# A hybrid decoder step on one core: the first FFN operands on two engines in another order, more products ahead of them, the last output parts in one contraction

## The chip, the core and the metric

One NeuronCore of a Trainium2 chip runs the whole program. The core has four engines that compute, each with its own queue of instructions that it works off in order: TensorE (PE; its weight loads are shown as PEld), VectorE (DVE), ScalarE (ACT) and GpSimd (POOL). SyncE (SP) issues nearly all transfers. Matrix products go into PSUM, eight banks of 512 fp32 columns per partition; everything else lies in SBUF.

The metric is the device time of one execution in microseconds. The profile is of one further execution, whose own time is given beside the median of the others.

## The reference

One layer on 2048 prompt tokens and 8 decode tokens, model width 1024, FFN width 2816:

```python
h = rmsnorm(x, g_mix) * (1.0 + scale_m) + shift_m
proj = h @ w_in                      # q, k, v, g_ret, x_lru, g_lru
...
mix = jnp.concatenate([ret_out, lru_out], axis=-1) @ w_out
x = x + gate_m * mix

h = rmsnorm(x, g_ffn) * (1.0 + scale_f) + shift_f
u = h @ w_up_conv
gv = h @ w_up_gate
uc, s_conv_ffn_new = causal_dwconv(u, s_conv_ffn, conv_ffn_w, conv_ffn_b)
f = (jax.nn.gelu(uc) * gv) @ w_down
x = x + gate_f * f
```

Between `proj` and `mix` stand four retention heads (a chunkwise recurrence, 128 tokens a chunk) and an RG-LRU over 512 channels. `scale`, `shift` and `gate` are `silu(c) @ w_ada + b_ada`. The recurrent states are outputs too, and a last `rmsnorm` follows.

## The kernel before

**Numbers.** Every fp32 factor of the large products is split into a high part (the value rounded to the type `fp32r`, by ACT) and a low part (the rest, a subtraction), and a product is three matmuls: high·high, high·low, low·high. This is `mm3` (lines 346, 347, 348); all three lines appear in the profile for every product. The split weights are made once, in the first token group, by `parts` (ACT line 277, POOL line 278), stored to DRAM and loaded from there by the later groups.

**Groups and blocks.** The tokens are worked in three groups of 688, 680 and 688 columns (the last has the 8 decode tokens), each cut in two blocks of 344 (or 340). Activations lie transposed: channels on partitions, tokens along the free dimension. A group runs: projection (`head(p)`, `lru(t)`), retention (`ret`, in steps between other work), output projection (`out_(p)`), the second norm (`norm2`), FFN up and gate products, down projection (`dn`).

**FFN up and gate by seven products.** For a pair of 128-column output tiles and the two token blocks, the 2×2 block product of weights (A11, A12 | A21, A22) and activations is done by seven block products instead of eight. With b11, b21 the two halves of the channels (k below 4 and above) in block 0, and c12, b22 those of block 1:

- t1 = c12 − b11, t2 = b22 − t1, t3 = t2 − b11, t4 = b21 − t2
- P1 = A11·b11, P2 = A12·b21, P5 = S1·t1, P6 = S2·t2, P7 = S3·t3, P3 = S4·b22, P4 = A22·t4

where S1 to S4 are sums of the A. P1 and P2 need block 0 alone. The others need both blocks. Some products are added up in one PSUM bank (`qx`: P1, P6, P7, P4; `qz`: P5, P3; `qy`: P2), and the sums are taken out by ACT or DVE (`keep` line 971, `up_out` lines 1001 and 1003, `gate_out` line 1038). There are 11 pairs of tiles for `w_up_conv` and 11 for `w_up_gate`. One product is four k-steps of `mm3`, 12 matmuls.

**Where the operands come from.** After the last output part of a block, `square` and `norm2` make the norm factor: squares on ACT (842), their sum on DVE (845), small matmuls (858), DVE (862), POOL (864), DVE (867), and matmuls that spread the factor over partitions (869). Then `operands1` (block 0) and `operands2` (block 1) copy the factor from PSUM (lines 901, 917) and make the operand tiles `op`. `h2` (883 to 890) applies norm, scale and shift: in way "v" DVE multiplies (889) and ACT adds the shift (890), in way "p" POOL multiplies (886) and ACT scales and shifts (887). `hilo` (892 to 894) makes high parts on ACT (893) and low parts on DVE or POOL (894), as its caller says. The differences are DVE's lines 938, 940, 946 and 949. `raw32` holds b11 and b21 in fp32 for them (tile `keep`).

**Order.** `group_items` writes out the order of the work as a list of items (weight keys, rate, function). `fetch` is called for the keys ahead of use, up to a weight of `LOOK` = 4 blocks, into a ring of 8 blocks (`wb`); raw weights go through 7 buffers (`wr`, `ws`). After each item, generators in `soon` and `bg` (norms, retention steps) are advanced by the item's rate. This order gives priorities; the framework then lays out each engine's queue by a simulated schedule, and on the chip each queue runs in that fixed order. Before the change the end of the output projection runs as 12 items of head 2 and LRU tile 2, then a drain of `bg`, then 8 items of head 3, 4 of head 2 and 8 of head 3. Each item (`down_item`) contracts one head and one LRU tile, 6 matmuls, and is added to x by DVE (820). In front of the rest of the FFN stand four products that need block 0 alone: P1 and P2 of pair 0, for up and gate.

**Pools.** `x` has nine large slots (x, hh, hl, rope, heads, operands), `t` ten tiles of one block, `f` twelve split tiles, `pm` three and `pt` five PSUM banks.

Of the kernel before, what the change touches and what calls it, by code (L numbers as in the profile page):

```python
# [16 lines left out]
P = 128  # L17
# [3 lines left out]
NB = 8  # L21
# [7 lines left out]
HOW0, HOW1, HOW2 = "vmvmvmvm", "pmpmpmpm", "vpvpvpvp"  # L29
# [59 lines left out]
def hybrid_step(ctx: ExitStack, tc: tile.TileContext, I, O):  # L89
# [194 lines left out]
    def fetch(key, r_=None, lo_on=G):  # L284
# [15 lines left out]
        elif kind == "w_down":  # L300

            units[key] = parts(key, block(), None if key in split else load_rows_of(kind, a, 512 * key[2]), lo_on)
        elif kind in ("w_in", "w_out"):
            both = []
            for h in range(2):
                r_ = None
                if key + (h,) not in split:
                    r_ = load_rows_of(kind, a, 512 * h) if kind == "w_out" else load_cols_of(kind, a, h)
                both.append(parts(key + (h,), block(), r_, lo_on))
            units[key] = [(both[k // 4][0][:, k % 4, :], both[k // 4][1][:, k % 4, :]) for k in range(KC)]  # L310
        else:
            fetch_operand(key)

    def fetch_operand(key):
# [25 lines left out]
        if i == 0 and nm in ("A11", "A12"):  # L340
# [83 lines left out]
    def fsplit(src, n, name):  # L424
        hi = fp.tile([P, BMAX], F32R, tag="f", name=name + "h")
        lo = fp.tile([P, BMAX], F32R, tag="f", name=name + "l")
# [17 lines left out]
    class Group:  # L444
        def __init__(g, gi):
# [7 lines left out]
            g.xt, g.rope = {}, None  # L453
            g.started, g.sq, g.cv, g.fft, g.up = set(), {}, {}, {}, {}
# [155 lines left out]
        def ret(g, p):  # L610
# [66 lines left out]
            g.mixt[p] = {b: fsplit(SG[:, b[0]:b[1]], b[1] - b[0], "mr") for b in g.blocks}  # L677
# [66 lines left out]


# [14 lines left out]
        def lru_g(g, t, b):  # L760
# [7 lines left out]
            g.mixt.setdefault(4 + t, {})[b] = fsplit(xc, n, "ml")  # L768
# [39 lines left out]
        def down_item(g, keys, parts, jg, b, m):  # L808
# [3 lines left out]
            for i, key in enumerate(keys):  # L812
                if key[0] == "w_down":
                    wh, wl = (v[:, m % 4, :] for v in units[key])
                else:
                    wh, wl = units[key][m]
# [21 lines left out]
        def square(g, b, k):  # L838
# [4 lines left out]
            if 0 < k < KC - 1:  # L843
                acc = g.sq[b][0]
                V.tensor_tensor(out=acc, in0=acc, in1=t0, op=ALU.add)
            else:
                g.sq.setdefault(b, []).append(t0)
# [33 lines left out]
        def h2(g, k, c, n, bc, out, how):  # L881

            A, B = modv[:, 4, k, 0:1], modv[:, 3, k, 0:1]
            xs, t0 = g.xk(k)[:, c:c + n], out[:, 0:n]
            if how == "p":
                G.tensor_tensor(out=t0, in0=xs, in1=bc[:, 0:n], op=ALU.mult)
                S.activation(out=t0, in_=t0, func=AF.Identity, scale=A, bias=B)
            else:
                V.scalar_tensor_tensor(out=t0, in0=xs, scalar=A, in1=bc[:, 0:n], op0=ALU.mult, op1=ALU.mult)
                S.activation(out=t0, in_=t0, func=AF.Identity, bias=B)  # L890

        def hilo(g, nm, k, src, eng):
            S.activation(out=g.hi(nm, k), in_=src, func=AF.Copy)  # L893
            eng.tensor_tensor(out=g.lo(nm, k), in0=src, in1=g.hi(nm, k).bitcast(F32), op=ALU.subtract)  # L894

        def operands1(g, b, ps):
# [3 lines left out]
            bc = ttile("bc")  # L900
            S.activation(out=bc[:, 0:n], in_=ps[:, 0:n], func=AF.Copy)
# [10 lines left out]
        def operands2(g, b, ps):  # L912
            n, np_ = g.n, g.npr(b)
            for v in ("t1", "b22", "t2", "t4"):
                g.op[v] = slot("op", F32R)
            bc = ttile("bc")
            S.activation(out=bc[:, 0:n], in_=ps[:, 0:n], func=AF.Copy)
            tails, t3s = [], []
            if np_ < n:
                for u in range(2):  # L920
# [403 lines left out]
```

## Time and profile before

| | |
|---|---|
| median of 3 runs | 2508.69 us (2506.72 to 2509.22) |
| the profiled execution, its own time | 2514.42 us |
| span of its instructions | 2512.3 us |
| mean granted clock of TensorE | 0.971 |
| instructions | 40048 |
| busy: PE, DVE, ACT, POOL | 2395.7, 1465.1, 877.4, 840.6 us |
| bytes moved | 523.96 MB, mean 209 GB/s |

The groups' entries into the FFN lie at about 380, 1195 and 2000 us after the span's start. A timeline row has start, duration, engine, line, operation, output<-input, shapes and count; in brackets stands how long the engine was idle before and what ended the idle time. A row of waits has the waiting engine, its tile and line, what it waited for, then the sum, the count and the longest. A row of one line's durations has minimum, median and maximum in ns.

### The profile page before, as it was taken

The numbers are of one execution on the slowest core, as the hardware profiler recorded it, in microseconds if no ns is written. First come the engines' busy times: TensorE is split into PE (matmuls) and PEld (weight loads), VectorE is DVE, ScalarE is ACT, GpSimd is POOL, SyncE is SP. The second block draws the span as 40 slices with busy tenths as digits, with TensorE's granted clock in tenths as the row PEclk, the third lists the DMA queues.
The fourth block names the chain that finished last, engine by engine and source line by source line (L and its number), as shares of the span: only waits on it lengthen the run. The fifth ranks groups of instructions, "written<-read, shape, count | busy, mean of one in ns | idle before, by whom it ended". The sixth has DMA issues, their size and how long they took to land. (4 is left out here: it accounts for less than half of the span.)

```text
span 2512.3 us, 40048 instructions
## 1 busy us (share of the span) xinstructions
PE 2395.7 (95%) x15145; PEld 2293.4 (91%) x15145; DVE 1465.1 (58%) x3121; ACT 877.4 (35%) x1944; POOL 840.6 (33%) x849
## 2 busy tenths in 40 slices
PE   5999996999999999999799999999999979999997
PEld 4988885999999999999699999989999879999997
DVE  3745577676667766567644434376565855454545
ACT  3423446544444443223422222243123442222222
POOL 2544547767666643222311010132222330101011
PEclk8999997999999999999799999999999989999999
DMA  9575654888878854332466666746433245666673
GB/s 342 170 267 192 202 194 165 310 292 291 301 281 302 322 196 140 130 117 95 138 233 233 223 241 218 247 170 196 135 124 129 90 157 211 242 218 236 217 245 129
DMA packets 227777, 523.96 MB, mean 209 GB/s; under 512 B 18493, under 2 KB 100553, under 8 KB 227577
## 3 DMA queue, kind: packets, MB, share of 16 engines
q1 hardware_dynamic: 226483, 520.65, 59.8%
q8 instruction: 119, 1.95, 0.3%
q10 hardware_dynamic: 974, 0.50, 0.1%
q14 instruction: 73, 0.60, 0.1%
q0 software_dynamic: 128, 0.26, 0.0%
HBM read 373.04 MB, written 148.42 MB: 208 GB/s over the span
## 5 line engine op out<-in xcount | busy, mean ns | idle before, releaser
L820 DVE SCALAR_TENSOR_TENSOR x<-down,mod,x 128x344 f32<-128x344 f32 (+2 forms) x720 | 401.0, 569 | 329.9 <-PE down L348 324.7
L428 POOL TENSOR_TENSOR ffl<-cv,ffh 128x344 fp32r<-128x344 f32 (+1 forms) x132 | 132.3, 1009 | 763.9 <-ACT ffh L427 707.9
L346 PE MATMUL proj<-hh,wb 128*128 128x344 f32 (+1 forms) x1152 | 377.5, 328 | 10.1 <-ACT bc L546 7.2
L348 PE MATMUL proj<-hh,wb 128*128 128x344 f32 (+1 forms) x1152 | 371.4, 322 | 0.0
L347 PE MATMUL proj<-hl,wb 128*128 128x344 f32 (+1 forms) x1152 | 370.9, 322 | 0.2 <-DVE hl L559 0.2
L346 PE MATMUL down<-ffh,wb 128*128 128x344 f32 (+1 forms) x1056 | 339.9, 328 | 13.9 <-DVE x L820 13.1
L347 PE MATMUL qx<-op,wb 128*128 128x344 f32 (+1 forms) x1056 | 343.3, 325 | 9.7 <-DVE op L894 6.6
L346 PE MATMUL qx<-op,wb 128*128 128x344 f32 (+1 forms) x1056 | 341.3, 325 | 10.3 <-ACT op L893 6.2
L348 PE MATMUL qx<-op,wb 128*128 128x344 f32 (+1 forms) x1056 | 340.4, 323 | 0.0
L347 PE MATMUL down<-ffl,wb 128*128 128x344 f32 (+1 forms) x1056 | 338.3, 321 | 0.0
L348 PE MATMUL down<-ffh,wb 128*128 128x344 f32 (+1 forms) x1056 | 337.9, 321 | 0.0
L278 POOL TENSOR_TENSOR wb<-wr,wb 128x512 fp32r<-128x512 f32 x170 | 231.8, 1374 | 159.1 <-ACT wb L277 145.0
L346 PEld LDWEIGHTS proj<-hh,wb 128*128 128x128 f32 x1152 | 217.5, 189 | 19.9 <-ACT bc L546 7.3
L347 PEld LDWEIGHTS proj<-hl,wb 128*128 128x128 f32 x1152 | 218.0, 189 | 2.6 <-DVE hl L559 0.7
L346 PEld LDWEIGHTS down<-ffh,wb 128*128 128x128 f32 x1056 | 198.6, 189 | 23.6 <-DVE x L820 22.4
L348 PEld LDWEIGHTS proj<-hh,wb 128*128 128x128 f32 x1152 | 217.6, 189 | 1.7 <-issue 0.9
L347 PEld LDWEIGHTS qx<-op,wb 128*128 128x128 f32 x1056 | 202.7, 192 | 13.8 <-DVE op L894 9.9
L346 PEld LDWEIGHTS qx<-op,wb 128*128 128x128 f32 x1056 | 202.4, 192 | 12.3 <-ACT op L893 6.8
L1023 DVE SCALAR_TENSOR_TENSOR cv<-u,vec,cv 128x344 f32<-128x344 f32 (+2 forms) x264 | 178.4, 696 | 56.9 <-ACT cv L1004 54.3
L348 PEld LDWEIGHTS qx<-op,wb 128*128 128x128 f32 x1056 | 202.5, 192 | 0.1
L347 PEld LDWEIGHTS down<-ffl,wb 128*128 128x128 f32 x1056 | 200.2, 190 | 0.0
L348 PEld LDWEIGHTS down<-ffh,wb 128*128 128x128 f32 x1056 | 200.1, 190 | 0.0
(281 smaller groups left out, 4827.0 us busy)
## 6 DMA issues: line engine op xcount, KB each, us to landing
wb<-w_in SPq DMA_DIRECT2D x96, 512.0 KB
wb<-w_up_conv_S SPq DMA_DIRECT2D x88, 512.0 KB
wb<-w_up_gate_S SPq DMA_DIRECT2D x88, 512.0 KB
wb<-w_down SPq DMA_DIRECT2D x88, 512.0 KB
wb<-w_up_conv_A SPq DMA_DIRECT2D x66, 512.0 KB
wb<-w_up_gate_A SPq DMA_DIRECT2D x66, 512.0 KB
w_in<-wb SPq DMA_DIRECT2D x48, 512.0 KB
w_up_conv_S<-wb SPq DMA_DIRECT2D x44, 512.0 KB
```

The lines of the kernel that those rows point to most:

```text
L278: lo_on.tensor_tensor(out=w[:, 512:1024], in0=src, in1=w[:, 0:512].bitcast(F32), op=ALU.subtract)
L346: T.matmul(out, wh, xh, start=first, stop=False, skip_group_check=more)
L347: T.matmul(out, wh, xl, start=False, stop=False, skip_group_check=more)
L348: T.matmul(out, wl, xh, start=False, stop=last, skip_group_check=more)
L428: G.tensor_tensor(out=lo[:, 0:n], in0=src, in1=hi[:, 0:n].bitcast(F32), op=ALU.subtract)
L820: V.scalar_tensor_tensor(out=xs, in0=q[:, 0:np_], scalar=modv[:, jg, m, 0:1], in1=xs, op0=ALU.mult, op1=ALU.add)
L1023: V.scalar_tensor_tensor(out=cv[:, 0:np_], in0=u[:, j:j + np_], scalar=cfw[:, j, ft:ft + 1], in1=cv[:, 0:np_], op0=ALU.mult, op1=ALU.add)
```

## The change

`operands1` and `operands2` no longer use POOL. DVE multiplies x by scale and by the factor, read where it lies in PSUM (`scaled`); the shift is added where the high part is made (ACT) and where the low part is made (DVE). The four t1 are made first, with their parts; then t2 and b22 for each k; then the parts of t3; then t4. All products with b11 and b21 of pair 0 and of pair 1 (P1, P2; eight instead of four) come ahead of those that need block 1, and those of pair 0 then run up and gate in turn: P5, P6, P3, P7 and P4. For pair 1, P1 is kept in SBUF and added to P5, P6 and P4 when they are taken out, so that its bank need not stay. In group 0 the 14 operand weights of pair 0 are split and stored between the last output items, and loaded again for use.

The outputs of heads 2 and 3 become one contraction of 12 matmuls, `out_((2, 3), …)`: eight items of block 0, then eight of block 1 in the order m = 4…7, 0…3. `w_out` is fetched by halves, one block a key; the first half is fetched twice for this contraction. `head(3)` moves ahead of `lru(2)`. The split mix tiles of head 3 and LRU tile 3 get a slot of their own (`home`). Copies and additions that free PSUM get a higher priority.

```diff
-HOW0, HOW1, HOW2 = "vmvmvmvm", "pmpmpmpm", "vpvpvpvp"
+HOW0, HOW1 = "vmvmvmvm", "pmpmpmpm"
...
-        if i == 0 and nm in ("A11", "A12"):
+        if i == 1 and nm in ("A11", "A12"):
             del pr[nm]
...
+        def home(g, p, j, b):
+            if p < H - 1:
+                return None
+            if g.mix is None:
+                g.mix = slot("mix", F32R)
+            return [g.mix[:, j + i, b[0]:b[1]] for i in range(2)]
...
-        def hilo(g, nm, k, src, eng):
-            S.activation(out=g.hi(nm, k), in_=src, func=AF.Copy)
-            eng.tensor_tensor(out=g.lo(nm, k), in0=src, in1=g.hi(nm, k).bitcast(F32), op=ALU.subtract)
+        def scaled(g, k, c, n, bc, out):
+            V.scalar_tensor_tensor(out=out[:, 0:n], in0=g.xk(k)[:, c:c + n], scalar=modv[:, 4, k, 0:1],
+                                   in1=bc[:, 0:n], op0=ALU.mult, op1=ALU.mult)
+
+        def hilo(g, nm, k, src, B=None):
+            hi, lo = g.hi(nm, k), g.lo(nm, k)
+            if B is None:
+                S.activation(out=hi, in_=src, func=AF.Copy)
+                V.tensor_tensor(out=lo, in0=src, in1=hi.bitcast(F32), op=ALU.subtract)
+            else:
+                S.activation(out=hi, in_=src, func=AF.Identity, bias=B)
+                V.scalar_tensor_tensor(out=lo, in0=src, scalar=B, in1=hi.bitcast(F32),
+                                       op0=ALU.add, op1=ALU.subtract)
...
         def operands1(g, b, bc):
...
             for k in range(KC):
-                r_ = g.raw32(k)
-                g.h2(k, b[0], n, bc, r_, HOW2[k])
-                g.hilo("b11" if k < 4 else "b21", k % 4, r_, V if HOW2[k] == "p" else G)
+                g.scaled(k, b[0], n, bc, g.raw32(k))
+                g.hilo("b11" if k < 4 else "b21", k % 4, g.raw32(k), modv[:, 3, k, 0:1])
                 yield
...
+            for k in range(4):
+                c12.append(second(k))
+                t1 = ttile("t1")[:, 0:n]
+                V.tensor_tensor(out=t1, in0=c12[k], in1=g.raw32(k), op=ALU.subtract)
+                g.hilo("t1", k, t1)
+                yield
...
+            for k in range(4):
+                c22, t2 = second(4 + k), g.raw32(k)
+                V.scalar_tensor_tensor(out=c12[k], in0=c22, scalar=dB[:, k:k + 1], in1=c12[k],
+                                       op0=ALU.add, op1=ALU.subtract)
+                V.scalar_tensor_tensor(out=t2, in0=t2, scalar=B[k], in1=c12[k], op0=ALU.add, op1=ALU.add)
+                g.hilo("t2", k, t2)
+                yield
+                g.hilo("b22", k, c22, B[4 + k])
+                yield
+            for k in range(4):
+                g.hilo("t3", k, c12[k])
+                yield
...
+            early = what in ("P1", "P2") and i < 2
+            q = g.product(st, (kind, i, left), right, bank, start or apart and what == "P6",
+                          psm if early and (apart or what == "P2") else pst)
...
-        for v in v3[:8] + v2[12:] + v3[8:]:
-            add(*v)
+        its = out_((2, 3), [(g.blocks[0], m) for m in range(KC)]
+                   + [(g.blocks[1], m) for m in (4, 5, 6, 7, 0, 1, 2, 3)], 2)
+        ahead = [(kind, 0, PRODUCTS[what][0]) for kind in (UP, GATE) for what in seq] if g.gi == 0 else []
+        for it in its:
+            out.append(it)
+            if ahead:
+                key = ahead.pop(0)
+                add([key], 0, units.pop, key)
+        for i in range(2):
+            for kind in (UP, GATE):
+                for what in ("P1", "P2"):
+                    quad(kind, i, what, 3)
         add([], 0, lambda: drain(soon))
+        for pair in (("P5",), ("P6",), ("P3",), ("P7", "P4")):
+            for kind in (UP, GATE):
+                for what in pair:
+                    quad(kind, 0, what)
...
-        return 2 if key[0] in ("w_in", "w_out", "w_ada") else 1
+        return 2 if key[0] in ("w_in", "w_ada") else 1
```

More of the change, by code (lines that the diff above doesn't have):

```diff
@@ L842, in square @@
             S.activation(out=t0, in_=g.xk(k)[:, b[0]:b[1]], func=AF.Square)
[L843 to L847, printed above, removed]
+            sq = g.sq.setdefault(b, [])
+            sq.append(t0)
+            if 1 < len(sq) and not last:
+                V.tensor_tensor(out=sq[0], in0=sq[0], in1=sq.pop(), op=ALU.add)
         def norm2(g, b):
@@ L910, in raw32, with operands2 @@
             return g.keep32[:, k % 4, BMAX * (k // 4):BMAX * (k // 4) + g.n]
-        def operands2(g, b, ps):
+        def operands2(g, b, bc):
             n, np_ = g.n, g.npr(b)
[L914 to L918, printed above, removed]
+            B = [modv[:, 3, k, 0:1] for k in range(KC)]
+            tails = []
             if np_ < n:
+                rb = bc[:, np_:n].unsqueeze(1).to_broadcast([P, 4, NB])
@@ L961, in product @@
+            yield
+            g.op["t4"] = slot("op", F32R)
+            for k in range(4):
+                g.hilo("t4", k, t4s[k])
+                yield
+        def product(g, st, key, nm, bank, start, tile):
             wh, wl = units.pop(key)
             if start:
-                st[bank] = pst("q" + bank)
+                st[bank] = tile("q" + bank)
             q = st[bank][:, 0:g.n]
@@ L967, in product, with keep, quad_item @@
             return q
[L969 removed]
+        def keep(g, q, name, more=None):
             t = ttile(name)
[L971 removed]
+            with tc.high_priority(offset=2 * HASTE):
+                if more is None:
+                    S.activation(out=t[:, 0:g.n], in_=q, func=AF.Copy)
+                else:
+                    V.tensor_tensor(out=t[:, 0:g.n], in0=q, in1=more[:, 0:g.n], op=ALU.add)
             return t
[L974 removed]
+        def quad_item(g, st, kind, i, what, out, apart):
             left, right, bank, start = PRODUCTS[what]
[L976 removed]
+            early = what in ("P1", "P2") and i < 2
+            q = g.product(st, (kind, i, left), right, bank, start or apart and what == "P6",
+                          psm if early and (apart or what == "P2") else pst)
+            p1 = st.get("p1")
             if what == "P1":
@@ L1037, in gate_out @@
             if more is not None:
-                V.tensor_tensor(out=more[:, 0:n], in0=q, in1=more[:, 0:n], op=ALU.add)
-                q = more[:, 0:n]
+                t = (ttile("gv") if stays else more)[:, 0:n]
+                with tc.high_priority(offset=2 * HASTE):
+                    V.tensor_tensor(out=t, in0=q, in1=more[:, 0:n], op=ALU.add)
+                q = t
             V.tensor_tensor(out=cv, in0=cv, in1=q, op=ALU.mult)
@@ L1154, in dn @@
             return its
+        both = [(b, m) for h in range(2) for b in g.blocks for m in range(4 * h, 4 * h + 4)]
+        UP, GATE = "w_up_conv", "w_up_gate"
+        seq = ("P1", "P5", "P6", "P2", "P7", "P3", "P4")
         head(0, g.gi == 0)
@@ L1189, in group_items @@
             d = dn(i - 1, both) if i < np_ - 1 else []
-            for n, (kind, what) in enumerate((kind, what) for kind in (UP, GATE) for what in seq):
+            some = [(kind, what) for kind in (UP, GATE) for what in seq if i > 1 or what not in ("P1", "P2")]
+            for n, (kind, what) in enumerate(some):
                 quad(kind, i, what)
-                take = 0 if n < 1 else 1 if n < 2 else 2
+                take = 0 if n < 1 else 1 if n < 2 and i > 1 else 2
                 out.extend(d[:take])
                 d = d[take:]
+            out.extend(d)
         if nxt is not None:
```

196 lines of the change are left out of this document (83 added, 113 removed).

## The prediction

> **What bounds the kernel.** I read the page first. TensorE is the bound nearly everywhere, and three places break it.
>
> ```profile
> PE   5999996999999999999799999999999979999997
> PEclk8999997999999999999799999999999989999999
> ```
>
> One character is a fortieth of the span, 62.8 us. PE falls to 6, 7 and 7 tenths in the slices that begin at 377, 1193 and 2010 us, and the granted clock falls with it. Those are the entries into the FFN of the three token groups. The windows view gives their size; the last row is a steady stretch for comparison.
>
> ```profile
> 380.00:440.00 60.00, 36.27 (x147) 30.63 (x146) 46.34 (x76) 36.63 (x85) 43.01 (x41) 0.69 0.45 158
> 1190.00:1250.00 60.00, 44.61 (x202) 39.48 (x201) 41.38 (x68) 30.63 (x70) 26.47 (x26) 0.74 0.38 133
> 2000.00:2060.00 60.00, 44.98 (x205) 39.80 (x204) 41.02 (x95) 30.40 (x70) 28.02 (x26) 0.77 0.40 137
> 1256.00:1316.00 60.00, 60.00 (x387) 60.00 (x387) 27.64 (x53) 15.57 (x40) 6.39 (x7) 1.00 0.67 226
> ```
>
> Columns: window, length, busy time and instructions of PE, weight loads, DVE, ACT, POOL, then granted clock, DMA share, GB/s. At full rate 387 matmuls pass in 60 us, 0.155 us each. So the three windows lose 60·(1−n/387): 37.2, 28.7 and 28.2 us, **94.1 us together**. That is all this change can win at its own place. Who PE waits for, in the waits view of 1190 to 1250:
>
> ```profile
> PE qz L346 <- ACT op L893: 5.9, 4, 3.6
> PE qx L347 <- DVE op L894: 3.3, 3, 1.3
> PE down L346 <- DVE x L820: 3.0, 1, 3.0
> PE qx L346 <- DMA wb<-w_up_conv_A: 1.3, 1, 1.3
> PE qz L347 <- DVE op L894: 1.2, 2, 0.7
> PE qz L346 <- DVE u L1003: 0.5, 1, 0.5
> ```
>
> Nearly all of it is the operand tiles `op` (high parts of line 893, low parts of 894). These waits sum to 15.2 us while 28.7 us are lost; the rest is the slow clock (0.74 granted). So a microsecond of wait costs about 1.9 here. The Trainium skill ("TensorE: Matmul & The Clock Gate", Part 1) says that an idle window of about 3.4 us halves the clock and that shorter gaps keep it up. By that rule only the 3.6 us wait of this list would cost more than itself; the window disagrees, so I keep 1.9. By the rule the waits that I forecast below would cost only themselves, and the sum would be some 15 us lower, 2447.
>
> **The chain, before.** Why are operands late? Two rows of the DVE and two of POOL, then the whole-run durations of three lines:
>
> ```profile
> 1217.23 0.51 DVE L946 TENSOR_TENSOR t<-t,keep 128x340 f32<-128x340 f32 x1
> ```
> ```profile
> 1224.35 1.22 DVE L949 TENSOR_TENSOR keep<-keep,t 128x340 f32<-128x340 f32 x1
> ```
> ```profile
> 1217.84 1.08 POOL L894 TENSOR_TENSOR op<-h,op 128x340 fp32r<-128x340 f32 x1 [3.12 <-ACT op L893]
> ```
> ```profile
> 1224.13 1.06 POOL L886 TENSOR_TENSOR h<-x,bc 128x340 f32<-128x340 f32 x1
> ```
> ```profile
> L889 DVE SCALAR_TENSOR_TENSOR keep<-x,mod,bc x12: 1060/1222/1351, 379.6 to 2003.3; 128x344 f32<-128x344 f32 x8, 128x340 f32<-128x340 f32 x4
> ```
> ```profile
> L820 DVE SCALAR_TENSOR_TENSOR x<-down,mod,x x720: 534/569/579, 151.3 to 2497.0; 128x344 f32<-128x344 f32 x90, 128x340 f32<-128x340 f32 x60, 128x336 f32<-128x336 f32 x30
> ```
>
> A DVE operation with both tensors in SBUF takes 0.51 us when POOL is idle and 1.22 us when POOL runs beside it. Line 820, with one operand in PSUM, never leaves 534 to 579 ns in 720 cases. The kernel before puts the operand work on DVE and POOL at once, so each slows the other.
>
> **What the change removes.** Per group POOL loses 4+4 multiplications (L886), 4+8+4 low parts (L894) and ACT the 16 affine steps of lines 887 and 890 that stood inside the chain. The copy of the norm factor out of PSUM (lines 901, 917) goes too; the factor is now read from PSUM.
>
> **What it adds.** DVE makes everything but the high parts. Per group: 16 `scaled` with the factor in PSUM, at line 820's 0.57 = 9.1 us; and 44 with SBUF operands (8 low parts of `operands1`; in `operands2` nine fours: t1, its low part, the difference of the halves, t2, four more low parts, t4) at 0.51 = 22.4 us when POOL is quiet. With block 1's eight L820 (4.6), six square sums (3.0), two norm chains (1.6) and the outputs of the four early P2 (5.3 at these prices): 46 us on DVE. To it come the times in which DVE waits for a norm:
>
> ```profile
> 1184.88 0.57 DVE L820 SCALAR_TENSOR_TENSOR x<-down,mod,x 128x340 f32<-128x340 f32 x1 [0.36 <-PE down L348]
> ```
> ```profile
> 1191.08 4.76 DVE L889 SCALAR_TENSOR_TENSOR keep<-x,mod,bc 128x340 f32<-128x340 f32 x4 [0.54 <-ACT bc L901]
> ```
> ```profile
> 1200.23 0.57 DVE L820 SCALAR_TENSOR_TENSOR x<-down,mod,x 128x340 f32<-128x340 f32 x1 [0.81 <-PE down L348]
> ```
> ```profile
> 1213.76 1.33 DVE L889 SCALAR_TENSOR_TENSOR h<-x,mod,bc 128x340 f32<-128x340 f32 x1 [0.66 <-ACT bc L917]
> ```
>
> From the end of a block's last addition to its first operand: 5.6 us for block 0, 13.0 us for block 1. The second is long because PE's order puts the small norm matmuls behind others; I keep it, and let half of it be filled with what is left of `operands1`: 46+5.6+6.5 = **58 us of DVE** from the end of block 0.
>
> **The cover.** In the same time PE has, in the new order, block 1's 8 outputs of 12 matmuls, 8 early products (P1, P2 of pairs 0 and 1; before, 4) and 10 late ones, 12 matmuls each: 312·0.155 = 48.4 us, and twice the norm's own matmuls:
>
> ```profile
> 371.81 1.40 PE L858 MATMUL bc<-ones,sq 128*128 128x2 f32 x12
> ```
> ```profile
> 377.09 0.80 PE L869 MATMUL bc<-dg,ones 128*128 128x128 f32 x6
> ```
>
> 4.4 us, so **53 us**. DVE ends about 5 us late; at 1.9 that is some 9 us lost, where 28 were. The first products, which waited for `b11` before, begin 15 us after block 0, with `b11` ready at about 12 (5.6, four times 0.57+0.51, and some L820 between): nothing is lost there. What is late next is t2, made beside `b22`, and then t4. The ten tiles of the `t` pool are a second limit: four first-block differences, two kept P1 and the outputs' tiles share them; if they run out, P6's copy and with it P7 wait, 0 to two products (3.7 us). I take 0. I take 8 us for groups 1 and 2 each, since pair 1's late products can fill gaps. Ends: 0 and 20.
>
> **Group 0** also splits weights:
>
> ```profile
> L278 POOL TENSOR_TENSOR wb<-wr,wb 128x512 fp32r<-128x512 f32 x170 | 231.8, 1374 | 159.1 <-ACT wb L277 145.0 <-DMA wr<-in_w_in 7.5 <-DVE x L820 4.4
> ```
> ```profile
> 440.00:500.00 60.00, 57.98 (x366) 57.34 (x366) 39.87 (x56) 31.36 (x70) 46.08 (x35) 1.00 0.86 305
> ```
> ```profile
> 340.00:380.00 40.00, 40.00 (x262) 33.71 (x261) 30.78 (x80) 15.14 (x37) 18.13 (x23) 1.00 0.53 174
> ```
> ```profile
> SPq L281 <- POOL wb L278: 49.9, 9, 21.4
> ```
>
> The change moves the 14 splits of pair 0 ahead, between the output items. That takes 14·1.37 = 19 us of POOL out of the operand stretch, but POOL still works there for pair 1 (46 of 60 us in the steady window): with POOL active 40% of the time the 44 operations take 0.51+0.4·0.71 = 0.79 each, 12 us more, and weight sums on DVE add about 5. So DVE is some 22 us late, less what the weights hold PE up meanwhile (next part); I take 18 us of wait and, at 1.5 a microsecond (between 1 and group 1's 1.9), 27 lost. Ends: 10 and 60.
>
> **Cost that I hide behind DMA.** The sizes are in the page's list of issues:
>
> ```profile
> wb<-w_out SPq DMA_DIRECT2D x32, 512.0 KB
> ```
> ```profile
> wr<-in_w_out SPq DMA_DIRECT2D x16, 256.0 KB
> ```
>
> The output weights' first half is loaded a second time, 4·0.5 MB a group. In groups 1 and 2 the DMA share is 0.38 and 0.40: hidden. The stores and loads go through SP's queue, which in 340 to 440 us stood 49.9 us behind POOL's splits (the SPq row); every load queued behind waits too. That falls on group 0 alone.
>
> **Cost of the merged outputs.** Matmuls stay the same in number; 16 additions a group go (16·0.57 on DVE, off the bound). But 12 items of `out_(2)`, 72 matmuls or 11 us, no longer stand between the last LRU products and the first use of head 3 and LRU tile 3:
>
> ```profile
> 1940.74 0.46 ACT L751 ACTIVATE xl<-proj 128x344 f32<-128x344 f32 x1 [3.32 <-PE proj L348]
> ```
> ```profile
> 1965.59 0.49 ACT L427 ACTIVATE mlh<-xc 128x344 fp32r<-128x344 f32 x1 [3.30 <-DVE xc L767]
> ```
> ```profile
> 1977.40 0.48 ACT L427 ACTIVATE mrh<-head 128x344 fp32r<-128x344 f32 x1
> ```
> ```profile
> 1957.53 0.41 PE L346 MATMUL down<-mrh,wb 128*128 128x344 f32 x1
> ```
> ```profile
> 1968.00:1984.00 16.00, 13.31 (x73) 11.29 (x73) 10.58 (x43) 1.97 (x6) 4.96 (x11) 0.82 0.20 71
> ```
>
> PE reaches the outputs at 1957.5; head 3's retention is ready at 1977.4, and 16 us from 1968 have 73 matmuls where 103 fit: up to 4.7 us lost. In the new order head 3 is projected before lru(2), 96 matmuls or 15 us earlier, so its retention ends near 1962, where PE arrives with 9 matmuls of cover per open bank. I charge +1.5 us a group, between −5 and +11 (all the cover gone).
>
> **Sum**, against the profiled execution (span 2512.3, time 2514.4): 94.1 becomes 27+8+8 = 43, a gain of 51; 4.5 back for the outputs: −46.5, 2468. The median of the runs is 5.7 us below the profiled one: **2462 us**.
>
> **Rivals.** (a) *Splitting ahead overloads group 0*: between the first output and the second load of half 0, SP has 8 output halves (0.77 MB with store), 12 operand blocks (0.52 stored, 7 raw reads of 0.26), six ada keys and four reloads, 19.6 MB; at 305/0.86 = 355 GB/s (the steady row) that is 55 us, where PE has 22 us of matmuls and the ada items, some 30. Less 8 us fetched early, 17 us of wait, 27 lost on top: 2489. For it: the SPq row. Against it: DMA stands at 0.53 there now, and operands ripen during the wait.
> (b) *More is hidden*: pair 1's products fill every gap, group 0 loses 10 and the others 0 to 2: 94−14 = 80 won, 2430.
> (c) *Slower: DVE alone is too slow.* Place: `operands2` of every group. Time from block 0's end is 36+44s, s being the price of an SBUF operation. It gives back the whole gain when DVE ends 31/1.9 = 16 us after the 53, at s = 0.76 for groups 1 and 2. With s at 1.22, as beside POOL, DVE takes 90 us, 37 late, and even at one microsecond lost for each it makes 111 lost for 94, with 4.5: 2530. For it: 60 DVE operations replace 36. Against it: POOL has only four `ff` splits left there.
> (d) *The planner undoes it*: PE's order is laid out by a simulated schedule; if it queues early products behind late operands, time stays within 0.2%.
>
> **Chances:** forecast 0.50 (2445 to 2480), (a) 0.15, (b) 0.18, (c) 0.11, (d) 0.06. A measurement of this kernel tells about 0.2%, 5 us, from no change. Faster 0.83, same 0.06, slower 0.11. The range, 2418 to 2504, reaches from just under (b) to the edge of (d), and leaves (c) out.
>
> **What would show it.** After the change: 60-us windows at the three entries with over 330 matmuls in groups 1 and 2 and about 270 in group 0; clock above 0.9; DVE operands at 0.5 to 0.57 us in groups 1 and 2, no `op` on POOL. Wrong if PE waits on DVE `op` sum to over 10 us in a later group, if PE `down` waits on `wb` in group 0 before its operands, or if the wait has moved to `down <- mrh/mlh` at the start of the merged outputs.

## The result, and the profile after

The changed kernel takes **2477.23 us** (median of 4 runs, 2473.31 to 2477.89); the kernel before, run beside it, takes 2508.95 (4 runs, 2506.72 to 2512.14). The ratio is 0.9869, with an interval of 0.9852 to 0.9886: 31.7 us faster. The forecast was 2462 in a range of 2418 to 2504: the direction and the range held, the size was 15 us too good.

The profiled execution took 2476.83 us. Its page begins:

```profile
span 2475.0 us, 40030 instructions
PE 2372.8 (96%) x15145; PEld 2275.1 (92%) x15145; DVE 1450.5 (59%) x3160; ACT 855.6 (35%) x1943; POOL 762.9 (31%) x777
```

PE has the same 15145 matmuls and bounds the kernel as before. Since each group's count of matmuls is the same in both kernels, three windows, cut at the first projection matmul of each group, show where the time went. Columns: the window and its length, busy us (count) of PE, PEld, DVE, ACT and POOL, granted clock, DMA share, GB/s. Before:

```profile
0.00:907.40 907.40, 843.89 (x5317) 781.49 (x5317) 588.88 (x1061) 408.42 (x872) 532.17 (x471) 0.97 0.73 254
907.40:1698.10 790.70, 769.66 (x4885) 752.50 (x4883) 424.26 (x890) 243.98 (x553) 160.12 (x194) 0.97 0.54 187
1698.10:2512.30 814.20, 782.11 (x4950) 759.43 (x4948) 452.00 (x1172) 225.04 (x519) 148.28 (x184) 0.97 0.52 179
```

After:

```profile
0.00:908.50 908.50, 843.01 (x5317) 780.34 (x5317) 582.83 (x1078) 400.15 (x872) 503.32 (x447) 0.97 0.75 264
908.50:1682.60 774.10, 760.42 (x4886) 744.97 (x4883) 417.98 (x904) 236.53 (x552) 137.32 (x170) 0.99 0.55 194
1682.60:2475.00 792.40, 769.34 (x4950) 749.82 (x4948) 449.66 (x1180) 218.91 (x519) 122.29 (x160) 0.99 0.53 186
```

Groups 1 and 2 are 16.6 and 21.8 us shorter; **group 0 is 1.1 us longer**. The whole gain lies in two groups of three.

The entries into the FFN, as windows of 60 us of after (same columns), against the 147, 202 and 205 matmuls of before:

```profile
352.00:412.00 60.00, 39.61 (x221) 34.10 (x221) 35.66 (x69) 28.80 (x63) 31.77 (x28) 0.82 0.87 304
1185.00:1245.00 60.00, 52.63 (x318) 49.50 (x317) 46.03 (x106) 24.53 (x60) 6.04 (x5) 0.97 0.61 218
1980.00:2040.00 60.00, 51.63 (x307) 48.43 (x306) 47.89 (x129) 24.98 (x63) 3.89 (x4) 0.97 0.63 222
```

At 387 matmuls per 60 us the entries of groups 1 and 2 now lose 10.7 and 12.4 us (28.7 and 28.2 before), at a granted clock of 0.97. Group 0's window has 74 matmuls more than before, but its hole begins earlier. Its last output matmul is the 2307th in both kernels, and up to it both have run the same matmuls. Cut there and 194 matmuls later, before:

```profile
0.00:380.90 380.90, 352.56 (x2307) 304.13 (x2307) 217.61 (x512) 147.47 (x295) 169.54 (x188) 0.97 0.68 229
380.90:449.20 68.30, 43.94 (x194) 38.20 (x194) 50.23 (x82) 42.03 (x97) 49.15 (x45) 0.73 0.50 177
```

After:

```profile
0.00:407.00 407.00, 359.81 (x2307) 308.28 (x2307) 225.05 (x529) 159.59 (x318) 182.51 (x198) 0.95 0.70 233
407.00:445.90 38.90, 32.63 (x194) 31.81 (x194) 34.05 (x75) 21.69 (x55) 13.07 (x10) 0.91 0.90 344
```

The stretch behind the outputs, where the hole of before lies, is 29.4 us shorter, and the outputs end 26.1 us later: **the hole has moved ahead, into the outputs**. Of the 26.1 us, 7.3 are PE being busy longer for the same matmuls; nearly all the rest are waits. PE's waits in 335 to 425 us of after (sum, count, longest):

```profile
PE bc L874 <- DVE dg L872: 8.1, 2, 4.2
PE down L344 <- DMA wb<-w_out: 4.2, 1, 4.2
PE ada L368 <- DMA wr<-in_w_ada: 3.2, 2, 1.6
PE down L344 <- ACT wb L277: 3.0, 1, 3.0
PE oT L653 <- DVE on L442: 2.7, 1, 2.7
```

The first row is the norm: one of its two waits lies among the outputs, the other behind them. Three rows, 10.4 us in all, are weights that were not there: output weights from DRAM, raw modulation weights, an output weight still being split. The last row is a retention step that is late among the merged outputs. No row names an operand `op`. In 1185 to 1245 us (group 1) the list is short; these are its four longest, and the first is a load:

```profile
PE qz L344 <- DMA wb<-w_up_conv_S: 1.9, 1, 1.9
PE qz L344 <- ACT op L895: 1.7, 1, 1.7
PE qx L345 <- DVE op L896: 1.2, 1, 1.2
PE qy L344 <- ACT p L991: 0.6, 1, 0.6
```

DVE's price for an operand, over all three groups, as minimum, median and maximum in ns of one line's runs:

```profile
L896 DVE TENSOR_TENSOR op<-t,op x24: 500/505/518, 417.4 to 2024.7; 128x344 fp32r<-128x344 f32 x16, 128x340 fp32r<-128x340 f32 x8
L899 DVE SCALAR_TENSOR_TENSOR op<-keep,mod,op x24: 561/569/573, 397.3 to 1988.0; 128x344 fp32r<-128x344 f32 x16, 128x340 fp32r<-128x340 f32 x8
L955 DVE SCALAR_TENSOR_TENSOR keep<-keep,mod,h x12: 568/570/1247, 427.6 to 2016.3; 128x344 f32<-128x344 f32 x8, 128x340 f32<-128x340 f32 x4
```

The first two rows are the quiet price in every group, group 0 included. The slow price of a DVE operation beside POOL, 1.22 us before, is left in one operation of line 955 a group, beside the one FFN subtraction that POOL makes there.

### The profile page after: what moved, and what is told of

Its sections match the earlier page's. It is cut to its first block, busy times and chain, and to the rows that moved or that the text cites. A ratio compares the mean times of both kernels' runs of the same rounds, so it can differ in the third digit from the quotient of the medians.

```text
span 2475.0 us, 40030 instructions
## 1 busy us (share of the span) xinstructions
PE 2372.8 (96%) x15145; PEld 2275.1 (92%) x15145; DVE 1450.5 (59%) x3160; ACT 855.6 (35%) x1943; POOL 762.9 (31%) x777
## 5 line engine op out<-in xcount | busy, mean ns | idle before, releaser
L826 DVE SCALAR_TENSOR_TENSOR x<-down,mod,x 128x344 f32<-128x344 f32 (+2 forms) x672 | 374.6, 568 | 329.4 <-PE down L346 324.7
L429 POOL TENSOR_TENSOR ffl<-cv,ffh 128x344 fp32r<-128x344 f32 (+1 forms) x132 | 135.1, 1030 | 811.9 <-ACT ffh L428 733.3
L345 PE MATMUL qx<-op,wb 128*128 128x344 f32 (+1 forms) x1056 | 337.9, 320 | 3.8 <-DVE op L896 3.6
L344 PE MATMUL qx<-op,wb 128*128 128x344 f32 (+1 forms) x1056 | 337.7, 321 | 2.6 <-ACT op L895 1.1
L346 PE MATMUL qx<-op,wb 128*128 128x344 f32 (+1 forms) x1056 | 336.7, 319 | 0.0
L345 PEld LDWEIGHTS qx<-op,wb 128*128 128x128 f32 x1056 | 199.0, 188 | 5.2 <-DVE op L896 5.2
L344 PEld LDWEIGHTS qx<-op,wb 128*128 128x128 f32 x1056 | 198.8, 189 | 4.5 <-ACT op L895 1.9
L346 PEld LDWEIGHTS qx<-op,wb 128*128 128x128 f32 x1056 | 198.8, 188 | 0.1
```

Of the source, the lines that this page charges most:

```text
L344: T.matmul(out, wh, xh, start=first, stop=False, skip_group_check=more)
L345: T.matmul(out, wh, xl, start=False, stop=False, skip_group_check=more)
L346: T.matmul(out, wl, xh, start=False, stop=last, skip_group_check=more)
L429: G.tensor_tensor(out=lo[:, 0:n], in0=src, in1=hi[:, 0:n].bitcast(F32), op=ALU.subtract)
L826: V.scalar_tensor_tensor(out=xs, in0=q[:, 0:np_], scalar=modv[:, jg, m, 0:1], in1=xs, op0=ALU.mult, op1=ALU.add)
```

## The experiments

**Theory A** at this point: groups 1 and 2 gained because DVE alone is fast enough and more products cover it; group 0 gained nothing because the weights split ahead of their use, the raw modulation weights (`w_ada`) and the second load of `w_out` share SP's queue just where the outputs run. **Rivals**: group 0's loss is still DVE's; the gain is the products' alone, or the operands' alone; the merged outputs cost what the early products gain.

The runs stood beside the kernel before in three batches, whose medians for it were 2510.6, 2512.6 and 2513.0 us. The time of each group in the profiled executions, cut as above (group 2 ends with the span). The groups' times come from one execution of each kernel: after and the six variants that change group 0 alone (no_ahead, noahead_ada, ahead_late, ada_early, no_reload, late_ada) run the same code in groups 1 and 2 and spread there by 3.5 and 2.2 us, so a smaller difference of a group tells nothing.

| run | median us | ratio to before, interval | group 0 | group 1 | group 2 |
|---|---|---|---|---|---|
| before | 2508.95 | | 907.4 | 790.7 | 814.2 |
| after | 2477.23 | 0.9869 (0.9852 to 0.9886) | 908.5 | 774.1 | 792.4 |
| operands_only | 2507.61 | 0.9985 (0.9972 to 0.9998) | 904.3 | 790.2 | 809.8 |
| cover_only | 2501.83 | 0.9956 (0.9941 to 0.9971) | 917.0 | 779.4 | 801.3 |
| four_early | 2495.89 | 0.9932 (0.9917 to 0.9946) | 911.9 | 780.2 | 799.2 |
| head3_back | 2488.28 | 0.9905 (0.9891 to 0.9920) | 911.0 | 781.1 | 797.0 |
| pool_lows | 2480.02 | 0.9873 (0.9856 to 0.9889) | 912.0 | 772.1 | 793.3 |
| no_ahead | 2475.12 | 0.9855 (0.9835 to 0.9875) | 905.5 | 773.3 | 793.9 |
| noahead_ada | 2474.72 | 0.9845 (0.9828 to 0.9861) | 908.1 | 772.8 | 792.5 |
| ahead_late | 2472.40 | 0.9846 (0.9821 to 0.9871) | 903.2 | 772.1 | 792.6 |
| ada_early | 2470.15 | 0.9836 (0.9815 to 0.9857) | 902.4 | 774.2 | 794.5 |
| no_reload | 2462.52 | 0.9803 (0.9788 to 0.9818) | 895.5 | 773.4 | 792.3 |
| late_ada | 2460.27 | 0.9788 (0.9773 to 0.9802) | 890.8 | 770.7 | 792.6 |

### One half of the change alone

*operands_only*: the kernel before, with the new `scaled`, `hilo`, `operands1` and `operands2` and nothing else.

```diff
-                g.h2(k, b[0], n, bc, r_, HOW2[k])
-                g.hilo("b11" if k < 4 else "b21", k % 4, r_, V if HOW2[k] == "p" else G)
+                g.scaled(k, b[0], n, bc, g.raw32(k))
+                g.hilo("b11" if k < 4 else "b21", k % 4, g.raw32(k), modv[:, 3, k, 0:1])
...
```

> The kernel before with the new operand making alone (ScalarE and VectorE, new order of t1, t2, b22, t3, t4); order of products and output parts as before. If the engines are what counts: DVE operand rows at 0.50 to 0.57 us in groups 1 and 2, entries of groups 1 and 2 shorter by 8 to 12 us each, 2485 to 2495 us. If the cover (more matmuls ahead) is what counts: 60 DVE operations for 36 with the same cover, 2503 to 2518 us.

Measured: 2507.61, ratio 0.9985 (0.9972 to 0.9998): nearly nothing. Its group 1, as a window and as PE's waits from 1185 to 1250:

```profile
1188.00:1248.00 60.00, 44.65 (x219) 41.94 (x218) 41.86 (x95) 24.36 (x58) 1.76 (x2) 0.83 0.42 149
```
```profile
PE qx L347 <- DVE op L891: 5.2, 2, 4.4
PE bc L858 <- DVE sq L845: 2.5, 1, 2.5
```

POOL is all but idle and DVE's operations are cheap, but 60 of them stand where 36 stood: DVE is busy for 41.9 us of the window as against 41.4 before, and 219 matmuls in the hole are hardly more than 202. What was cheaper for one operation was spent on their number.

*cover_only*: the changed kernel with the operands of before (`h2` in its two ways, the low parts partly on POOL, the old order).

```diff
-HOW0, HOW1 = "vmvmvmvm", "pmpmpmpm"
+HOW0, HOW1, HOW2 = "vmvmvmvm", "pmpmpmpm", "vpvpvpvp"
...
-                g.scaled(k, b[0], n, bc, g.raw32(k))
-                g.hilo("b11" if k < 4 else "b21", k % 4, g.raw32(k), modv[:, 3, k, 0:1])
+                r_ = g.raw32(k)
+                g.h2(k, b[0], n, bc, r_, HOW2[k])
+                g.hilo("b11" if k < 4 else "b21", k % 4, r_, V if HOW2[k] == "p" else G)
...
```

> The changed kernel with the operand making of before (DVE and POOL together, old order of t1, t2, b22, t4, t3); order of products and merged outputs stay. The operands alone gave 3 us. Theory C (the cover alone gives the gain): 2477 to 2485 us. Theory B (both are needed: a faster chain matters only once enough matmuls stand ahead of it): 2490 to 2503, with waits of qz and qx on op of over 6 us in groups 1 and 2, since the parts come off DVE and POOL at 1.0 to 1.2 us each.

Measured: 2501.83. Groups 1 and 2 gain 11.3 and 12.9 us by it, and group 0 loses 9.6. The entry of group 1:

```profile
1185.00:1245.00 60.00, 50.76 (x295) 46.89 (x293) 42.94 (x77) 28.69 (x67) 25.03 (x24) 0.91 0.40 144
```
```profile
PE qz L344 <- ACT op L898: 4.5, 3, 3.0
PE qx L345 <- DVE op L899: 1.3, 1, 1.3
PE down L344 <- DVE x L826: 1.3, 1, 1.3
```

The cover halves the hole with the old operands behind it: 60·(1−295/387) = 14.3 us lost for 28.7, while POOL works 25 us there. In groups 1 and 2 the halves alone give 0.5+11.3 = 11.8 and 4.4+12.9 = 17.3, together 16.6 and 21.8: some 5 us a group more than their sum, a little over the spread. The operands are worth 0.5 and 4.4 us without the cover and 5.3 and 8.9 us behind it. The operands' half changes the engines, the number of operations and their order at once; which of these counts behind the cover was not separated.

### How much a product is worth

*four_early*: only pair 0's P1 and P2 come early, four products as before; pair 1's run with pair 1.

```diff
-        for i in range(2):
-            for kind in (UP, GATE):
-                for what in ("P1", "P2"):
-                    quad(kind, i, what, 3)
+        for kind in (UP, GATE):
+            for what in ("P1", "P2"):
+                quad(kind, 0, what, 3)
...
```

> The changed kernel with four early products instead of eight (P1 and P2 of pair 1 back in their place). By the sum of the prediction the cover falls by 4 times 12 matmuls, 7.5 us, and DVE is later by as much: at 1.0 to 1.9 us lost a microsecond, 7 to 14 us in each of three groups, less where group 0 waits for weights anyway: 2492 to 2505 us. If the merged outputs give most of the gain: 2477 to 2484.

Measured: 2495.89, and 3.4, 6.1 and 6.8 us more than after, group by group. That is below the 7 to 14 us a group that were expected. Group 1's entry has 280 matmuls and a clock of 0.89:

```profile
1185.00:1245.00 60.00, 49.24 (x280) 45.49 (x279) 44.50 (x101) 23.05 (x55) 5.50 (x4) 0.89 0.46 166
```
```profile
PE qx L344 <- ACT op L895: 2.9, 1, 2.9
PE qx L345 <- DVE op L896: 2.9, 2, 2.1
PE qz L344 <- ACT op L895: 1.7, 1, 1.7
```

The 48 matmuls taken away are 7.4 us of cover (60/387 each): **0.8 to 0.9 us lost for each microsecond of cover** in groups 1 and 2. This is not the price of a wait: all waits in this window rise from 7.1 us in after to 10.6, and what it loses from 10.7 us to 16.6, which is 1.7 for each further microsecond of wait, near the forecast's 1.9. Less than half of the cover taken away came back as wait.

### The merged outputs and head 3

*head3_back*: `head(3)` behind `lru(2)` again.

```diff
-        head(3)
         lru(2)
+        head(3)
         lru(3)
```

> The changed kernel with head(3) behind lru(2) again, as before the change, so that its retention starts four items (96 matmuls, 15 us) later while the merged outputs follow at once. If the 11 us of cover that the merging took away are paid for by the earlier head, as the prediction says: waits at the start of the merged outputs, +4 to +11 us a group, 2489 to 2510 us. If retention has slack anyway: 2475 to 2481.

Measured: 2488.28, just under the range expected; 2.5, 7.0 and 4.6 us more than after, group by group. PE's waits of this kernel in 1140 to 1190 us, ahead of the outputs of group 1:

```profile
PE kvT L653 <- DVE sT L626: 3.3, 2, 1.9
```

The same stretch of after has one wait of 0.9 us. With head 3 projected ahead of LRU tile 2 the retention steps lie beside the LRU's matmuls; without it PE waits for them at the end. In group 1, from its start to its last output matmul, before takes 292.8 us, head3_back 296.5 and after 288.5. The merged contraction is free in this group only with the move. The merging by itself, with the old order and the early products kept, was not tried.

### Who makes the low parts

*pool_lows*: the low parts of t3 and t4, the last ones wanted, on POOL.

```diff
-                V.tensor_tensor(out=lo, in0=src, in1=hi.bitcast(F32), op=ALU.subtract)
+                (G if nm in ("t3", "t4") else V).tensor_tensor(out=lo, in0=src, in1=hi.bitcast(F32), op=ALU.subtract)
```

> The changed kernel with the low parts of t3 and t4 (8 of DVE's 60 operations a group) on POOL again. If POOL beside DVE costs more than it takes over: DVE rows with SBUF operands near 1.0 to 1.2 us in that stretch instead of 0.5, P7 and P4 later, 2481 to 2492 us. If DVE's number of operations is what counts: 2468 to 2475. Between them neither is told apart.

Measured: 2480.02; its ratio's interval overlaps after's: the theories are not told apart by the time. The rows do show the price. In group 1 (1200 to 1240 us) of this run, DVE's groups of one form:

```profile
L899 DVE SCALAR_TENSOR_TENSOR op<-h,mod,op 128x340 fp32r<-128x340 f32 x4 | 4.2, 1058 | 0.0
L896 DVE TENSOR_TENSOR op<-keep,op 128x340 fp32r<-128x340 f32 x4 | 2.6, 680 | 0.0
L953 DVE SCALAR_TENSOR_TENSOR h<-h,dB,h 128x340 f32<-128x340 f32 x4 | 2.9, 731 | 0.0
```

In after the same three groups take 567, 504 and 568 ns. Eight subtractions fewer on DVE (8·0.5 = 4 us) are paid for by 0.49·4+0.18·4+0.16·4 = 3.3 us on those that stay; line 955 gives 0.7 us back, its one slow operation of after being a quick one here. Group 1 gains 2.0 and group 2 loses 0.9, both within the spread: no gain or loss from moving these parts to POOL is shown.

### Group 0: weights

*no_ahead*: nothing split ahead; group 0's late products kind by kind, so that each split is made once, at use.

```diff
-        if i == 1 and nm in ("A11", "A12"):
+        if i < 2 and nm in ("A11", "A12"):
...
-        ahead = [(kind, 0, PRODUCTS[what][0]) for kind in (UP, GATE) for what in seq] if g.gi == 0 else []
+        ahead = [(kind, 0, PRODUCTS[what][0]) for kind in (UP, GATE) for what in seq] if g.gi < 0 else []
...
-        for pair in (("P5",), ("P6",), ("P3",), ("P7", "P4")):
+        late = (("P5",), ("P6",), ("P3",), ("P7", "P4"))
+        if g.gi == 0:
+            late = (("P5", "P6", "P7", "P3", "P4"),)
+        for pair in late if g.gi else ():
...
+        for kind in (UP, GATE) if g.gi == 0 else ():
+            for what in late[0]:
+                quad(kind, 0, what)
```

> The changed kernel without the 14 splits ahead in group 0; there the late products of pair 0 run up first, then gate, as before. Theory W (group 0 is held up by weights: raw buffers and SP's queue behind the splits): the merged outputs of group 0 lose their 10 us of waits on wb and wr, but the splits come back beside the operands; 2470 to 2477 us. Rival D (group 0 is held up by operands that POOL's splits slow down, so that splitting ahead is what helps): 2483 to 2495 us. Groups 1 and 2 unchanged within 2 us.

Measured: 2475.12, not told apart from after by the time; group 0 at 905.5, 3 us below after. So the splits ahead are not 27 us on top: the net of taking them out is 3. But the net is made of two large terms. Group 0 cut at its last output matmul and 194 matmuls later, as above (us):

| run | to the last output | next 194 matmuls | rest of group 0 |
|---|---|---|---|
| before | 380.9 | 68.3 | 458.2 |
| after | 407.0 | 38.9 | 462.6 |
| no_ahead | 384.1 | 56.6 | 464.8 |
| ahead_late | 397.0 | 45.2 | 460.9 |
| ada_early | 400.5 | 39.5 | 462.4 |
| late_ada | 393.4 | 37.2 | 460.2 |

Without the splits ahead the outputs end 22.9 us earlier, 3.2 us behind before's, and PE's waits there on weights fall from 10.4 us to 1.3. The next 194 matmuls take 17.7 us longer: PE's waits on operands come to 6.1 us there, which in after had ripened during the wait for weights, and 3.0 us are waits on the splits that now stand beside them.

*ahead_late*: the splits only behind block 1's outputs, two an item.

```diff
-            if ahead:
-                key = ahead.pop(0)
-                add([key], 0, units.pop, key)
+            if ahead and it[3][0] == g.blocks[1]:
+                for key in [ahead.pop(0) for _ in range(2) if ahead]:
+                    add([key], 0, units.pop, key)
```

> The changed kernel with the 14 splits placed behind block 1's outputs, two an item, so that the second half of the output weights is not queued behind them. Theory W: the waits of down on w_out in the first eight items go (7 us), 2470 us, or 2473 if the second load of the first half waits longer instead. Rival D: within 2 us of 2477, or later, up to 2485, since more splits then run beside the operands.

Measured: 2472.40, group 0 at 903.2. Its outputs have one long wait, 9.5 us of `down` for `w_out`: the second load, the case for which 2473 was expected.

*ada_early*: the modulation items (`ada_mm`, each with a 256 KB load of `w_ada`) all spread at the rate of the first, so that they end before the outputs.

```diff
-                    c += (0.75 if todo[0][0] == 2 else 0.5) * it[1]
+                    c += 0.75 * it[1]
```

> The changed kernel with the modulation weights (w_ada) spread at 0.75 of an item instead of 0.5, so that they are done before the merged outputs of group 0 begin and leave the raw buffers to w_out and the operands. Theory W: the waits on wr<-in_w_ada (3 us) and part of those on w_out go, 2468 to 2472 us. Rival D: 2477 within 2 us; if DMA is the limit everywhere in group 0, the waits turn up earlier, 2477 too.

Measured: 2470.15, group 0 at 902.4. Neither of the two edits alone is told apart from after: the ratios' intervals overlap.

*late_ada*: both edits together.

> Both shifts of group 0's weight work: splits behind block 1's outputs and w_ada spread at 0.75. If they relieve different waits (w_out behind splits; raw buffers held by w_ada): 2463 to 2467 us. If both relieve the same one: 2469 to 2472.

Measured: **2460.27**, ratio 0.9788 (0.9773 to 0.9802), clear of after and 3 us below the range expected; group 0 at 890.8. Alone the two brought 5.3 and 6.1 us of group 0, together 17.7, and 13.6 of these lie in the outputs. Two windows show what was freed, asked for the tile `ada` alone (its PE time and count, then clock, DMA share and GB/s of the core). After:

```profile
300.00:340.00 40.00, 3.75 (x24) 1.00 0.56 185
340.00:400.00 60.00, 6.72 (x48) 0.84 0.69 237
```

late_ada:

```profile
300.00:340.00 40.00, 1.89 (x16) 1.00 0.91 308
340.00:400.00 60.00, 0.00 (x0) 0.88 0.74 271
```

In after, 48 of the modulation matmuls and their loads stand between the outputs, while DMA was only 0.56 busy just before. In late_ada DMA works at 0.91 ahead of the outputs, and PE's waits on weights there fall from 10.4 us to 2.3, on `w_out`. Its outputs still end 12.5 us later than before's; 3.7 us of waits on an LRU tile and 3.7 on earlier additions stand there, which are no weights. The busy strip of DMA in 300 to 412 us (40 slices of 2.8 us, in tenths), of after and of no_ahead:

```profile
DMA  7752580797064600041967919998997499999999
```
```profile
DMA  9571680895062300571699999999999999924049
```

After has three slices of zero from 339 to 348 us. Its 237 GB/s from 340 to 400 us are far from the 355 that the prediction took for a busy strip: for a part of that time SP's queue stood. Its waits in 330 to 412 us of after, two rows, and its issues around the zeros (start, duration of the issuing):

```profile
SPq L281 <- POOL wb L278: 26.3, 14, 6.4
SPq L262 <- PE oT L653: 11.1, 1, 11.1
```
```profile
335.29 1.48 SPq L268 DMA_DIRECT2D wr<-in_w_up_conv  x2
347.96 1.15 SPq L262 DMA_DIRECT2D wr<-in_w_ada  x2
```

From 336.8 to 348.0 SP issues nothing: at its head stands a load of modulation weights for a raw buffer that PE has to release, and every load and store behind it waits too. (The row names the transpose `oT`, which PE runs right behind modulation matmuls of 347.3.) Another 26.3 us go to stores of splits that POOL has not finished.

A standing queue alone is not the loss, though. no_ahead's strip has zeros at the same place, its SP waits 13.8 us for modulation matmuls, and its outputs end only 3.2 us later than before's; late_ada's SP waits longer for POOL's splits, 32.5 us, and is faster. The numbers fit the splits' added traffic through a queue that stands. Up to the last output after's DMA moves 94.8 MB, no_ahead's 89.1, at 233 and 232 GB/s: 5.7 MB more, which at this rate are 25 us, where 22.9 were measured. late_ada moves 97.6 MB by 393.4 us, at 248. Whether more raw buffers, or a second issuing queue, would do the same was not tried.

*noahead_ada*: no_ahead with the earlier modulation.

> No splits ahead in group 0 and w_ada spread at 0.75. If raw buffers are what is short in the merged outputs of group 0: 2467 to 2471 us. If the splits beside the operands take the gain: 2473 to 2477.

Measured: 2474.72, the same as no_ahead: a miss. The outputs of no_ahead lose only 3.2 us, so there is little for the earlier modulation to win; it is worth something only where the splits ahead use the room it leaves.

*no_reload*: late_ada with group 0's merged outputs by halves of `w_out` (the order `both`, m = 0…3 for both blocks, then 4…7), which needs no second load there. The splits ahead stand behind the outputs of the second half.

```diff
-        its = out_((2, 3), [(g.blocks[0], m) for m in range(KC)]
+        its = out_((2, 3), both if g.gi == 0 else [(g.blocks[0], m) for m in range(KC)]
...
```

> The variant with both shifts (2460 us) with group 0's merged outputs by halves (four of block 0, four of block 1, then the other halves), so that the first half of the output weights is loaded once in group 0; the splits ahead stand behind the outputs of the second half. If the second load is what still holds group 0: 2452 to 2458 us. If the later end of block 0 (four items, 7.5 us) leaves the operands too late: 2463 to 2472.

Measured: 2462.52, overlapping late_ada; group 0 is 4.7 us longer in the profiled execution. PE's wait of 2.3 us for `w_out` is gone and the outputs end 9.4 us earlier than late_ada's, but the 194 matmuls from there take 48.1 us instead of 37.2, with 5.8 us of waits for the loads of operand weights (3.6 and 2.2). Block 0's norm also starts later in this order. What the second load costs by itself was not separated from the other order.

## Why the prediction came out as it did

**The size, by its terms.** On the profiled executions the sum was 2468 and the time 2476.8.

| | change forecast (us) | measured |
|---|---|---|
| group 0 (37.2 to 27, outputs +1.5) | −8.7 | +1.1 |
| group 1 (28.7 to 8, outputs +1.5) | −19.2 | −16.6 |
| group 2 (28.2 to 8, outputs +1.5) | −18.7 | −21.8 |

Groups 1 and 2 come out together at −38.4 against −37.9. **The mis-sized term is group 0's**, "18 us of wait and, at 1.5 a microsecond …, 27 lost": it is 9.8 us off, the other groups +2.6 and −3.1. The rest of the way to 2477.2 is the 5.7 us that were taken off for the median; after's own profiled execution lies at its median (2476.83 against 2477.23), so that there was nothing to take off.

**What failed in that step.** The term has two wrong parts, and they run against each other. Behind the outputs it charged DVE beside a POOL busy 40% of the time, 0.79 us an operation, 27 us lost. Line 896 never took over 518 ns, no wait of PE in group 0 names an operand, and the 194 matmuls behind the outputs take 38.9 us where 30 is full rate (194·60/387): 9 lost. In the outputs it charged 1.5 us and gave the weights no price of their own ("less what the weights hold PE up meanwhile"); there 26.1 were lost, 10.4 of them as waits for weights: the sign that the prediction had named under "wrong if". Without the splits ahead 22.9 of the 26.1 go (no_ahead), with splits and modulation placed otherwise 13.6 (late_ada). That group 0 came out only 9.8 us off is luck: the two parts are off by 18 and by 25. cover_only says from the other side that it is not the operands: the cover's part, with the splits ahead in it, costs group 0 9.6 us, the operands' part gains 3.1. Another 4.4 us are lost in the rest of group 0, spread over its FFN; where is open.

**Rival (a)** had the place and the mechanism right (SP's queue, weights in group 0), and even its 27 us lost, against the 22.9 that go without the splits. It was wrong in "on top": the operands ripened meanwhile, which it had put down against itself. Its rate was wrong too, 355 GB/s from a busy strip where 237 were reached. The same transfers placed otherwise cost 13.6 us less up to the last output (late_ada). **Rival (b)** needed group 0 to lose 10; no version did that, though late_ada's group 0 is 16.6 us shorter than before's. **Rival (c)**, DVE alone too slow, falls by the rows at 0.50 to 0.57 us; operands_only shows what was true in it: on its own, the DVE version is no gain. **Rival (d)** falls with the result.

**The steps that held.** DVE's price: 0.50 to 0.57 us for all but one operation a group. The sum took 0.51 for all 44 with SBUF operands; 24 of them are scalar_tensor_tensor and took 0.57, which makes some 2 us a group more. DVE late by a little only: PE's waits for `op` in group 1's entry sum to 3.9 us, 1.7 on ACT's high parts and 2.2 on DVE's low ones. The merged outputs of groups 1 and 2: +1.5 a group was charged, and they were a gain. From a group's start to its last output matmul after is 4.3 and 7.6 us shorter than before (292.8 to 288.5, 310.9 to 303.3), a part of it before's own hole, which began ahead of the last output; the 194 matmuls behind give 13.9 and 13.3 of the 20.7 and 20.2 that were forecast for the entry. These two errors run against each other as well, so that the sums of groups 1 and 2 are in part luck. head3_back puts 7.0 and 4.6 us on the move of head 3, inside the bounds of −5 to +11. The second load of `w_out` hidden in groups 1 and 2: no wait of theirs names it. The signs were a little too good: 318 and 307 matmuls where "over 330" were named, 221 where about 270 were.

**The price of a wait.** The 1.9 us per microsecond of wait came from a hole at clock 0.74. In the shallow holes of after it is 10.7/7.1 = 1.5 (PE's waits in group 1's entry sum to 7.1), in group 2's 12.4/8.3 = 1.5, in four_early's 16.6/10.6 = 1.6. The price falls a little as the hole gets shallow. What the forecast had no price for is how much wait a microsecond of missing cover makes: less than half of one in four_early.

The Trainium skill ("TensorE: Matmul & The Clock Gate", Part 1) gives an idle window of about 3.4 us as what halves the clock, and also tells of a kernel in which frequent short idle times between matmuls did it. Two windows here agree with the second: four_early's longest wait in group 1's entry is 2.9 us at a granted clock of 0.89, after's 1.9 us at 0.97. operands_only, with one of 4.4 us, is at 0.83. The forecast by the first rule alone, 2447, was farther off than the one by rows.

## What to carry to other kernels

A hole in front of the bounding engine has two sides, the work that fills it and the work that ends it, and the halves of a change may be worth less one by one than together (here 0.5 and 11.3 us of group 1, but 16.6 together): price them together, and do not take missing cover for wait. Compare by stretches with equal counts of the bounding engine's instructions: this shows that one group of three had gained nothing, and, cut at the last output, that its hole had moved ahead of the window laid over it. A net of 3 us can be 22.9 won and 17.7 lost. Where loads are brought forward into one in-order queue, ask what each issue waits for before adding up bytes; spreading the same loads and splits otherwise, around a stretch whose DMA was only 0.69 busy, gave group 0 17.7 us.

## What the runs showed of the hardware that was not expected

POOL can be the one that is slowed. In after's group 0, four subtractions of DVE keep their 0.51 us while POOL's subtraction for the FFN, 1030 ns in the mean of 132, takes 2.5 us beside them; the fifth DVE operation beside it, line 955, then takes 1.25:

```profile
432.90 2.52 POOL L429 TENSOR_TENSOR ffl<-cv,ffh 128x344 fp32r<-128x344 f32 x1 [14.61 <-ACT ffh L428]
```
```profile
432.83 0.93 DVE L896 TENSOR_TENSOR op<-h,op 128x344 fp32r<-128x344 f32 x2
```
```profile
434.54 1.25 DVE L955 SCALAR_TENSOR_TENSOR keep<-keep,mod,h 128x344 f32<-128x344 f32 x1
```

In pool_lows, with POOL's operations back to back, both are slow: three on POOL take 3.40 us, and two on DVE, which start beside the third of them and beside the next one, 2.35.

```profile
1225.69 3.40 POOL L896 TENSOR_TENSOR op<-h,op 128x340 fp32r<-128x340 f32 x3 [16.28 <-ACT op L895]
```
```profile
1228.24 2.35 DVE L899 SCALAR_TENSOR_TENSOR op<-h,mod,op 128x340 fp32r<-128x340 f32 x2
```

So here a series of POOL operations takes turns with DVE at about 1.15 us each, and a lone one among DVE's waited for four of them and then cost the fifth 0.68 us. Line 955's one slow operation a group, beside such a lone one, is all that the work left on POOL costs the operands. The Trainium skill ("SBUF — State Buffer", "Who interferes with whom") says that such a pair of operations locks a shared port, that whoever issues first has it for the whole instruction, and that the other blocks. That either engine can be the one that waits agrees with these rows; a lock for whole instructions would make a pair take 0.57+0.92 = 1.5 us, by the quiet durations of after (line 899; POOL's line 429 in a quiet place, below), and 1.15 were measured.

```profile
1235.48 0.92 POOL L429 TENSOR_TENSOR ffl<-cv,ffh 128x340 fp32r<-128x340 f32 x1 [8.58 <-ACT ffh L428]
```
